# Queries projected in float32 and normalised at the output, no packing of the latents, own buffers for the gates' tanh

## The chip, the cores and the metric

The kernel runs on one core of one Trainium2 chip. The metric is the device time of one execution in microseconds (us). Several runs are timed, and one further execution is recorded by the hardware profiler; its rows are the views shown below. Engines are named as in the profile: PE is TensorE's matmul, PEld its weight load, DVE is VectorE, ACT is ScalarE, POOL is GpSimd, SP is SyncE. "SPq" and "ACTq" are the sequencers of SP and ACT that issue DMAs.

## The reference, cut to what matters

One backbone layer over 256 latent tokens and 256 context tokens: a SwiGLU FFN, two token mixers in parallel (a gated DeltaNet and a Mamba-2 SSD, each in both directions), their gated merge and an output projection, then a second FFN on the latents alone. The part that is changed is the queries and what uses them:

```python
qkv = jax.nn.silu(conv(qkv, gdn_conv_w))
q, k, v = jnp.split(qkv, [GDN_QK, 2 * GDN_QK], axis=-1)
q = l2norm(q.reshape(b, n, GDN_HEADS, GDN_DK)) * GDN_DK ** -0.5      # t * rsqrt(sum(t*t) + EPS)
k = l2norm(k.reshape(b, n, GDN_HEADS, GDN_DK))
...
qk = jnp.einsum('bnhid,bnhjd->bnhij', q, k) * decay                  # both uses of q are linear in it
q_in = q * jnp.exp(g)[..., None]
...
ya = (rmsnorm(o, gdn_norm_g) * jax.nn.silu(za)).astype(dt).reshape(b, n, GDN_V)
...
merged = jax.nn.sigmoid(ga) * (ya @ w_branch_gdn) + jax.nn.sigmoid(gb) * (yb @ w_branch_mb)
return merged @ w_out
```

The output o of a head and token is linear in that token's query, and rmsnorm then divides by the root of o's mean square plus EPS. So the query's norm can be left out if EPS is multiplied by 128 times (the query's sum of squares + EPS).

## The kernel before

Activations lie with channels on the 128 partitions and tokens along the row: NT = 512 tokens (256 context, then NL = 256 latent). A weight tile `raw` (128 x 1024 float32, four buffers, each loaded by SP) is used in one of two ways.

- **`proj`** (matmuls at lines 215, 216 and 217, "mm3"): ACT casts `raw` to `whi` (line 200), DVE takes the rest as `wlo` (line 204), and for each of 8 channel blocks PE runs three matmuls of type fp32r: hH x whi, hL x whi and hH x wlo. Keys, values, x (`wxs`) and the B matrices go this way over 512 tokens, queries over the 256 latents.
- **`projf`** (line 616): 8 matmuls in plain float32 on `hF`, straight from `raw`. The profile records each of them as two matmuls. The gates g (`wg`), C and zA go this way.

After a projection, `conv_silu` makes the convolution of five taps: a copy into `cbuf` and a scaled start on ACT, four steps on DVE (line 635), tanh on ACT (line 638), a last step on DVE (line 640). `l2` then normalises keys and queries: transposes to `l2t` (line 866), squares on ACT, sum on DVE (line 874, for the queries), the power on POOL (line 351), product `l2n` on DVE (line 877), transposes back to `l2b` (line 880), copy on ACT (line 881).

The middle of the program, from about 434 us on, is written as the list `PLAN` in `mixer` and reordered by a scheduler that goes by priorities (the numbers ahead of a slash) and its own simulated times; so each engine's order of instructions comes out of it and moves when any piece changes. Tiles of a tag share a fixed number of buffers: `tZ` holds the gates' `gth`, z's tanh tiles and the tiles `dtx` and `dte` of the time steps' softplus (`dts`, lines 741 to 754, 841 to 856); `tL` holds, among others, `dtz`, `dtg`, `rows_a` and `RB`.

The names in this stretch: `keys` (line 887 on) makes for each of the 8 heads the Gram matrix `pg` (PE, line 901), copies it to `kb` (ACT, line 903) and stores it by `Gsd<-kb` (SP, line 904); `N<-Gsd` (SP, line 910) reads blocks of it back, after every second head. `elim` multiplies N by the decay `D` (line 968) and inverts the triangular blocks in 30 steps on DVE (`etmp`, line 972, and `N`, line 975), stores them (`Tsd`, line 978), and `merge` reads them back as `TD` and `TT` (SP, line 1107) and begins with the transposes `pTx` (PE, line 1131). `merge` also needs decays `RA` and `RB`, loaded by SP (lines 1104 and 1112), subtracted on DVE (line 1119), exponentiated on ACT (line 1121) and multiplied into `Lm` on POOL (line 1122). The chain over chunks (`chain_step`), the queries, B and the x projections run between the merges.

Of the kernel before, what the change touches and what calls it, by code (L numbers as in the profile page):

```python
# [6 lines left out]
F32 = mybir.dt.float32  # L7
F32R = mybir.dt.float32r
AF = mybir.ActivationFunctionType
ALU = mybir.AluOpType  # L10
# [4 lines left out]
P = 128  # L15
D = 1024
KD = 8
NL = 256
NT = 512
FF = 2816  # L20
MF = 22
EPS = 1e-6
# [7 lines left out]
NCV = 2  # L30
POOLC = lambda t, s: False
PLAN = """10/k3 block_decay k6 5/elim 18/g5 13/dts 20/v2 g10 v7 13/m0 14/m1 13/chain_start s0 s1 m2 m3 22/q9
    B_part 27/x17 25/lat_h 22/C_part 30/zB5 g17 zA9 chain_out 13/s2 s3 14/gdn_norm 15/ssd_pre h40 51/y0 gdn_out y1 70/mb_out"""
NG = 5
GQ = 0
SSE = "gvg"
# [59 lines left out]
class Ks:  # L96

    def __init__(self, kern, nk, n, name, dt=F32R, lazy=False, tag="s4"):
        w = min(nk, 1024 // n)
        self.new = lambda: (kern.s4 if tag == "s4" else kern.tt)([P, w, n], name, dt)  # L100
        self.t = [None if lazy else self.new() for _ in range(-(-nk // w))]
        self.w = w

    def __getitem__(self, k):
        if self.t[k // self.w] is None:
            self.t[k // self.w] = self.new()
        return self.t[k // self.w][:, k % self.w]


class Packed:  # L110

    def __init__(self, t):
        self.t = t

    def __getitem__(self, k):
        j = k // 2
        return self.t[j // 2 * 2][:, k % 2, NL * (j % 2):NL * (j % 2) + NL]


class Ring:  # L120
# [19 lines left out]
class Kernel:  # L140
# [812 lines left out]
    @staticmethod  # L953
    def bc(ap, n, w):
        return ap.rearrange("p (h o) -> p h o", o=1).to_broadcast([ap.shape[0], n, w])
# [38 lines left out]
            self.tok_major(s, self.vsc[:, :, h].rearrange("t p c -> p t c"), "vt")  # L994
            yield

    def lat_h(self):

        nc = self.nc
        for i, X in enumerate((self.hH, self.hL)):  # L1000
            for j in (0, 2):
                dst, src = X.t[j][:, :, NL:NT], X.t[j + 1].bitcast(F32)[:, :, 0:NL]
                if i:
                    nc.vector.tensor_copy(dst, src)
                else:
                    nc.scalar.copy(dst, src)
        self.hH, self.hL = Packed(self.hH.t), Packed(self.hL.t)

    def q_gen(self):
        qT = self.qT = Ks(self, 8, NL, "qT", F32)  # L1010
        for h in range(8):
            acc = self.proj("wq", h, self.hH, self.hL, NL, QL[h % len(QL)])
            s = self.conv_silu(acc, NL, self.cwg[:, h])
            self.l2(s, NL, qT[h], 128.0, 128.0 * EPS)
            yield

    def xs_gen(self):
# [54 lines left out]
    def g_gen(self):  # L1072
        for m in range(16):
            acc = self.projf("wg", m)
            th = self.t2([P, NL], "gth", tag="tZ")
            self.nc.scalar.activation(th, acc, AF.Tanh, scale=0.5)  # L1076
            self.nc.scalar.dma_start(self.gsc[m], th)
            yield
# [187 lines left out]
    def gdn_norm(self):  # L1266

        nc, V = self.nc, self.nc.vector
        o, bc = self.o, self.bc
        rs = self.const([P, 2, 8], "ors")  # L1270
        for t in range(2):
            sq = getattr(self, OSQ)([P, 8, P], "osq")
            nc.scalar.activation(sq, o[t], AF.Square)
            V.tensor_reduce(out=rs[:, t], in_=sq, op=ALU.add, axis=AX.X)
        self.rsqrt(rs, rs, 1.0 / 128, EPS)
        for t in range(2):
            V.tensor_tensor(o[t], o[t], bc(rs[:, t], 8, P), op=ALU.mult)

# [354 lines left out]
```

## Time and profile before

| | us |
|---|---|
| three timed runs | 1347.86, 1344.52, 1350.04 (median 1347.86) |
| profiled execution, device time | 1350.37 |
| its span, first to last instruction | 1348.6 |
| mean granted TensorE clock | 0.973 |
| PE busy | 1267.5 (94%) |
| DVE busy | 977.1 (72%) |
| ACT busy | 508.9 (38%) |
| POOL busy | 172.4 (13%) |

The span is 1.8 us shorter than the device time of the same execution, and that execution is 2.5 us above the median of the timed runs. By the stages of the program: the first FFN until about 408 us; keys, gates, values and the elimination from 434 to 599.5 us (called stage B below); merges, chain, queries, B and x from 599.5 to 872 us (stage C); the SSD from 872 to 1004 us (stage D); gated output norms to 1056 us; branch and output projections and the second FFN to the end.

In the views, a row gives the line of the kernel's text, the engine, the operation and the tiles as out<-in, how often (x), busy time, and the idle time of the engine before it with what ended that wait.

### The profile page before, as it was taken

Reading aid. Unit: us, or ns where it says so; the run is one execution under the profiler, and the core shown is the slowest. Engines: PE = TensorE matmul, PEld = TensorE weight load, DVE = VectorE, ACT = ScalarE, POOL = GpSimd, SP = SyncE. Lnnn points to the kernel's source line nnn. Section 1 sums busy time; section 2 is a strip of 40 time slices with the busy share of each in tenths; the row PEclk is TensorE's granted clock in tenths of the full one; section 3 lists DMA queues with packets and bytes.
Section 4 is the critical chain, followed back from the end, with each engine's and each line's share of the span. In section 5 each row is a group of like instructions: output and inputs, shape, how many; then the busy total and the mean of one; then the engine's idle time right before and its main releaser. Section 6 shows DMA issues by size and latency. Waiting matters only on the chain.

```text
span 1348.6 us, 21052 instructions
## 1 busy us (share of the span) xinstructions
PE 1267.5 (94%) x8064; PEld 1083.8 (80%) x8064; DVE 977.1 (72%) x1692; ACT 508.9 (38%) x948; POOL 172.4 (13%) x130
## 2 busy tenths in 40 slices
PE   5889999999999997989998999998899899999997
PEld 3668888888899885779887888844468899999997
DVE  7998587646667966888778687997873466866565
ACT  3432122212236652345323565522223345544333
POOL 4200000000010231000122111333421001000000
PEclk9999999999999998999998999998999899999999
DMA  9256367636633398755542254554446556655552
GB/s 360 94 173 217 126 199 249 223 117 229 209 110 104 103 237 178 215 165 165 171 120 89 95 177 141 155 184 131 162 148 214 182 181 192 199 185 180 184 182 84
DMA packets 133016, 230.24 MB, mean 171 GB/s; under 512 B 46706, under 2 KB 78898, under 8 KB 132788
## 3 DMA queue, kind: packets, MB, share of 16 engines
q1 hardware_dynamic: 106240, 211.43, 49.7%
q10 hardware_dynamic: 26676, 17.47, 4.2%
q8 instruction: 63, 1.03, 0.3%
q14 instruction: 37, 0.30, 0.1%
HBM read 207.79 MB, written 21.07 MB: 170 GB/s over the span
## 4 chain that ended last, share of the span: by engine, by line
PE 63%; issue 17%; DVE 11%; DMA 7%; ACT 1%; POOL 1%; SPq 0%; ACTq 0%; DVEq 0%; POOLq 0%
PE acc L215 16%; PE acc L216 15%; PE acc L217 15%; PE acc L616 4%; PE acc L1054 2%; DVE junk L277 1%; DVE Es L1431 1%; DVE wlo L204 1%; PE pn L1232 1%; DMA zAsc<-zth 1%; DVE hL L440 1%; DMA Es<-asd 1%; DVE Es L1442 1%; PE pS L1258 1%; DMA raw<-in_wv 1%
## 5 line engine op out<-in xcount | busy, mean ns | idle before, releaser
L200 ACT CAST whi<-raw 128x1024 fp32r<-128x1024 f32 (+1 forms) x208 | 214.4, 1033 | 434.1 <-PE acc L216 369.4
L215 PE MATMUL acc<-hH,whi 128*128 128x512 f32 (+1 forms) x976 | 343.4, 358 | 17.2 <-ACT whi L200 8.3
L216 PE MATMUL acc<-hL,whi 128*128 128x512 f32 (+1 forms) x976 | 344.7, 355 | 4.6 <-DVE hL L440 4.6
L217 PE MATMUL acc<-hH,wlo 128*128 128x512 f32 (+1 forms) x976 | 343.3, 354 | 0.0
L204 DVE TENSOR_TENSOR wlo<-raw,whi 128x1024 fp32r<-128x1024 f32 (+1 forms) x208 | 254.4, 1225 | 93.3 <-ACT whi L200 92.0
L215 PEld LDWEIGHTS acc<-hH,whi 128*128 128x128 f32 x976 | 187.4, 192 | 43.0 <-ACT whi L200 8.6
L216 PEld LDWEIGHTS acc<-hL,whi 128*128 128x128 f32 x976 | 187.0, 192 | 30.5 <-DVE hL L440 6.9
L217 PEld LDWEIGHTS acc<-hH,wlo 128*128 128x128 f32 x976 | 186.3, 191 | 23.7
L277 DVE CUSTOM_DVE_ANT_0 junk<-wadat,cs 128x1024 f32<-128x1024 f32 x80 | 97.7, 1221 | 41.6 <-DMA wadat<-in_wadaT 40.9
L216 PE MATMUL acc<-aL,whi 128*128 128x256 f32 (+1 forms) x384 | 122.9, 323 | 0.0
L217 PE MATMUL acc<-aH,wlo 128*128 128x256 f32 (+1 forms) x384 | 122.3, 323 | 0.0
L215 PE MATMUL acc<-aH,whi 128*128 128x256 f32 (+1 forms) x384 | 122.3, 323 | 0.0
L616 PE MATMUL acc<-hF,raw 128*128 128x256 f32 x416 | 97.7, 391 | 14.6 <-ACT gth L1076 14.6
L635 DVE SCALAR_TENSOR_TENSOR cv<-cbuf,cc,cv 128x512 f32<-128x512 f32 (+1 forms) x144 | 102.0, 719 | 4.3 <-ACT cv L633 2.4
L616 PEld LDWEIGHTS acc<-hF,raw 128*128 128x128 f32 x416 | 80.3, 196 | 28.3 <-ACT gth L1076 16.0
L216 PEld LDWEIGHTS acc<-aL,whi 128*128 128x128 f32 x384 | 73.0, 190 | 5.7
L215 PEld LDWEIGHTS acc<-aH,whi 128*128 128x128 f32 x384 | 72.6, 190 | 5.7 <-DVE xc L572 0.2
L217 PEld LDWEIGHTS acc<-aH,wlo 128*128 128x128 f32 x384 | 72.7, 190 | 5.6
L382 POOL TENSOR_TENSOR sqa<-sqa,sqb 128x256 f32<-128x256 f32 x12 | 11.8, 981 | 430.5 <-ACT sqb L380 427.6
L572 DVE SCALAR_TENSOR_TENSOR xl<-acc,hg,xl 128x256 f32<-128x256 f32 x64 | 30.3, 481 | 47.3 <-PE acc L217 46.8
L1054 PE MATMUL acc<-raw,hF 128*128 128x512 f32 x128 | 59.4, 606 | 0.0
L1054 PEld LDWEIGHTS acc<-raw,hF 128*128 128x128 f32 x128 | 25.0, 197 | 30.2 <-issue 29.3
(398 smaller groups left out, 2082.3 us busy)
## 6 DMA issues: line engine op xcount, KB each, us to landing
raw<-in_wgu SPq DMA_DIRECT2D x76, 512.0 KB, 4.1
wadat<-in_wadaT SPq DMA_DIRECT2D x56, 512.0 KB, 4.1
raw<-in_wdn SPq DMA_DIRECT2D x44, 512.0 KB, 3.6
wada<-in_wada SPq DMA_DIRECT2D x16, 512.0 KB, 9.0
raw<-in_wg SPq DMA_DIRECT2D x16, 512.0 KB, 4.3
raw<-in_wxs SPq DMA_DIRECT2D x16, 512.0 KB, 3.4
Es<-asd SPq DMA_DIRECT2D x16, 512.0 KB, 4.3
raw<-in_wzB SPq DMA_DIRECT2D x16, 512.0 KB, 4.2
```

Source lines behind the costliest of these rows:

```text
L200: nc.scalar.copy(hi, raw)
L204: engs[i % len(engs)].tensor_tensor(lo[:, c:c + w], raw[:, c:c + w], hi[:, c:c + w].bitcast(F32), op=ALU.subtract)
L215: mm(acc, wh, xh, start=start, stop=False)
L216: mm(acc, wh, xl, start=False, stop=False)
L217: mm(acc, wl, xh, start=False, stop=stop)
L277: self.nc.vector.tensor_tensor_reduce(out=self.junk, in0=w, in1=self.cs[s], scale=1.0, scalar=0.0, op0=ALU.mult, op1=ALU.add, accum_out=out)
L440: nc.vector.scalar_tensor_tensor(out=hL[k][:, a:b], in0=u, scalar=sh[:, s:s + 1], in1=hH[k].bitcast(F32)[:, a:b], op0=ALU.add, op1=ALU.sub ...
L572: nc.vector.scalar_tensor_tensor(out=xs, in0=acc[:, NL * s - g0:NL * s - g0 + NL], scalar=hg[s][:, m:m + 1], in1=xs, op0=ALU.mult, op1=ALU ...
L616: self.nc.tensor.matmul(acc, w[:, k * P:k * P + P], self.hF[:, k], start=k == 0, stop=k == KD - 1)
L635: nc.vector.scalar_tensor_tensor(out=u3, in0=buf[:, 0:R, j:j + 64], scalar=cw[:, j:j + 1], in1=u3, op0=ALU.mult, op1=ALU.add)
L1054: nc.tensor.matmul(accs[t], self.hF[:, k, sl], w[:, wsl], start=k == 0, stop=k == 7)
L1232: nc.tensor.matmul(pn[:, j], TT[d][:, 4 * q + j], vt[q][:, j], start=True, stop=True)
```

## The change

- `q_gen` uses `projf` instead of `proj` (no `whi`, no `wlo`), writes the convolution's result straight into `qT`, and leaves `l2` out. In its place ACT squares `qT`, two matmuls against a column of ones give the sum of squares of each token (`pqs`), and ACT copies the two columns into `qs`.
- `gdn_norm` multiplies `qs` by 128 EPS, adds 128 EPS squared, adds the result to o's mean square, and POOL takes the power -1/2 as before.
- `lat_h` and `Packed` go: they copied the latents' halves of hH and hL into one tile, which the queries' projection alone read.
- `gth` leaves the tag `tZ` and gets two buffers of its own.

```diff
-    B_part 27/x17 25/lat_h 22/C_part 30/zB5 g17 zA9 chain_out 13/s2 s3 14/gdn_norm 15/ssd_pre h40 51/y0 gdn_out y1 70/mb_out"""
+    B_part 27/x17 22/C_part 30/zB5 g17 zA9 chain_out 13/s2 s3 14/gdn_norm 15/ssd_pre h40 51/y0 gdn_out y1 70/mb_out"""
...
-class Packed:
-
-    def __init__(self, t):
-        self.t = t
-
-    def __getitem__(self, k):
-        j = k // 2
-        return self.t[j // 2 * 2][:, k % 2, NL * (j % 2):NL * (j % 2) + NL]
...
-    def lat_h(self):
+    def q_gen(self):
 
         nc = self.nc
-        for i, X in enumerate((self.hH, self.hL)):
-            for j in (0, 2):
-                dst, src = X.t[j][:, :, NL:NT], X.t[j + 1].bitcast(F32)[:, :, 0:NL]
-                if i:
-                    nc.vector.tensor_copy(dst, src)
-                else:
-                    nc.scalar.copy(dst, src)
-        self.hH, self.hL = Packed(self.hH.t), Packed(self.hL.t)
-
-    def q_gen(self):
         qT = self.qT = Ks(self, 8, NL, "qT", F32)
+        self.qs = self.const([P, 2, 8], "qs")
         for h in range(8):
-            acc = self.proj("wq", h, self.hH, self.hL, NL, QL[h % len(QL)])
-            s = self.conv_silu(acc, NL, self.cwg[:, h])
-            self.l2(s, NL, qT[h], 128.0, 128.0 * EPS)
+            acc = self.projf("wq", h)
+            self.conv_silu(acc, NL, self.cwg[:, h], qT[h])
+            sq = self.t2([P, NL], "qsq")
+            nc.scalar.activation(sq, qT[h], AF.Square)
+            ps = self.smp([P, 2], "pqs")
+            for t in range(2):
+                nc.tensor.matmul(ps[:, t:t + 1], sq[:, t * P:t * P + P], self.ones[:, 0:1], start=True, stop=True)
+            nc.scalar.copy(self.qs[:, :, h], ps)
             yield
...
             acc = self.projf("wg", m)
-            th = self.t2([P, NL], "gth", tag="tZ")
+            th = self.tp.tile([P, NL], F32, tag="gth", bufs=2, name="gth")
             self.nc.scalar.activation(th, acc, AF.Tanh, scale=0.5)
...
-        self.rsqrt(rs, rs, 1.0 / 128, EPS)
+
+        e = self.const([P, 2, 8], "oeps")
+        V.tensor_scalar(out=e, in0=self.qs, scalar1=128 * EPS, scalar2=128 * EPS * EPS, op0=ALU.mult, op1=ALU.add)
+        V.scalar_tensor_tensor(out=rs, in0=rs, scalar=1.0 / 128, in1=e, op0=ALU.mult, op1=ALU.add)
+        mh = self.mhalf.rearrange("p (a o) -> p a o", o=1).to_broadcast([P, 2, 8])
+        nc.gpsimd.tensor_tensor(rs, rs, mh, op=ALU.pow)
```

From line 110 on, line numbers are lower by 10 in the changed text, and by 14 between `q_gen` and `gdn_norm`. Besides what the diff says, the scheduler gives every engine another order from the keys on. Three places matter for what follows.

On DVE, around the start of the elimination (`N<-N,D`), before. `cv` is a value's convolution, `dt`, `dte`, `dtx` and `dtg` belong to the softplus of the time steps, `etmp` and `N` are the elimination:

```order
L751 SCALAR_TENSOR_TENSOR dt<-dt,dtz 128x256
L968 TENSOR_TENSOR N<-N,D 128x1024 x2
L635 SCALAR_TENSOR_TENSOR cv_3344<-cbuf_3238,cc,cv_3344 128x512
L752 SCALAR_TENSOR_TENSOR dt<-dt,dte 128x256
L972 TENSOR_TENSOR etmp<-N 128x60
L635 SCALAR_TENSOR_TENSOR cv_3344<-cbuf_3238,cc,cv_3344 128x512
L754 SCALAR_TENSOR_TENSOR dt<-dt,dtx 128x256
L975 TENSOR_TENSOR N<-N,etmp 128x2x30
L845 TENSOR_TENSOR dtg<-dt,alogs 128x256
L972 TENSOR_TENSOR etmp<-N 128x116
L975 TENSOR_TENSOR N<-N,etmp 128x2x29x2
L640 SCALAR_TENSOR_TENSOR cv_3344<-cv_3344 128x512
```

The same place of the changed kernel (`gt` is the last copy of `dts`, `RB` the first merge's decay):

```order
L843 COPY gt<-pcd 128x256
L625 SCALAR_TENSOR_TENSOR cv_3343<-cbuf_3237,cc,cv_3343 128x512
L1105 TENSOR_TENSOR RB<-gcA,RB 128x256
L625 SCALAR_TENSOR_TENSOR cv_3343<-cbuf_3237,cc,cv_3343 128x512
L1105 TENSOR_TENSOR RB<-RB,gcA 128x256
L625 SCALAR_TENSOR_TENSOR cv_3343<-cbuf_3237,cc,cv_3343 128x512 x2
L1105 TENSOR_TENSOR RB<-gcA,RB 128x256
L630 SCALAR_TENSOR_TENSOR cv_3343<-cv_3343 128x512
L1105 TENSOR_TENSOR RB<-RB,gcA 128x256
L625 SCALAR_TENSOR_TENSOR cv_3344<-cbuf_3238,cc,cv_3344 128x512 x4
L630 SCALAR_TENSOR_TENSOR cv_3344<-cv_3344 128x512
L958 TENSOR_TENSOR N<-N,D 128x1024 x2
```

The rest of the softplus, its copies `gc` and `gt`, the whole of two convolutions and two of three pairs of `RB` now stand ahead of the elimination, where before they stood inside it; behind `N<-N,D` come sixteen rows of `etmp` and `N` alone. In all, twelve convolution steps of line 635 stand inside the elimination instead of fourteen, one pair of `RB` instead of three, and six `wlo` as before.

On PE, from the values' first transposes (`ptm`) to the first merge's `pTx`, before. `acc<-hF,raw` are the gates' matmuls, and behind x48 come 120 matmuls of values:

```order
L985 MATMUL ptm<-ident,cv_3343 128x128 x4
L616 MATMUL acc<-hF,raw 128x256 x16
L848 MATMUL pcd<-dtg,UT 128x4x32
L848 MATMUL pcd<-dtg,LT 128x4x32
L849 MATMUL pcd<-dtg,ones 128x256
L616 MATMUL acc<-hF,raw 128x256 x8
L855 MATMUL prow<-ident,gc 128x128
L616 MATMUL acc<-hF,raw 128x256 x48
...
L985 MATMUL ptm<-ident,cv_3344 128x128 x4
L985 MATMUL ptm<-ident,cv_3343 128x128 x4
L1131 MATMUL pTx<-ident,TD 32x32 x8
```

And of the changed kernel, where behind x74 come the same 120 matmuls of values, and then 20 more:

```order
L891 MATMUL pg<-kT 128x128 x4
L606 MATMUL acc<-hF,raw 128x256 x4
L975 MATMUL ptm<-ident,cv_3343 128x128 x4
L606 MATMUL acc<-hF,raw 128x256 x74
...
L975 MATMUL ptm<-ident,cv_3343 128x128 x4
L975 MATMUL ptm<-ident,cv_3344 128x128 x4
L205 MATMUL acc<-hH_3012,whi 128x512
L206 MATMUL acc<-hL_3014,whi 128x512
...
L206 MATMUL acc<-hL_3098,whi 128x512
L975 MATMUL ptm<-ident,cv_3343 128x128 x3
L1117 MATMUL pTx<-ident,TD 32x32 x8
```

`pcd` and `prow` of the softplus have moved up, ahead of the last `pg`, and 20 of the 24 matmuls of the last value's projection, which stood behind `pTx`, stand ahead of it.

On SP, from the sixth head's store of the Gram matrix to the last read of N, before (these are the DMAs that SP issues, in their order):

```order
L904 DMA Gsd<-kb_3352 128x4x128
L606 DMA raw<-in_wg 128x1024
L910 DMA N<-Gsd 16x64x32 x2
L904 DMA Gsd<-kb_3350 128x4x128
L1196 DMA kTt<-kTsc 128x1024 x2
L904 DMA Gsd<-kb_3351 128x4x128
L910 DMA N<-Gsd 16x64x32 x2
```

And of the changed kernel:

```order
L894 DMA Gsd<-kb_3352 128x4x128
L1098 DMA RB<-gsd 64x8x32 x4
L900 DMA N<-Gsd 16x64x32 x2
L1098 DMA RB<-gsd 64x8x32 x2
L894 DMA Gsd<-kb_3350 128x4x128
L1098 DMA RB<-gsd 64x8x32 x2
L1182 DMA kTt<-kTsc 128x1024 x2
L894 DMA Gsd<-kb_3351 128x4x128
L900 DMA N<-Gsd 16x64x32
L596 DMA raw<-in_wg 128x1024
L900 DMA N<-Gsd 16x64x32
```

Eight loads of `RB` have moved up between the last three stores of the Gram matrix, and a load of weights stands between the two halves of the last read of N.

## The prediction

> **What bounds the kernel now.** I read the table of engines first (in the table above: PE 94% of the span, DVE 72%), then busy time by stage, the waits of the stage with most idle PE time, and the chain of work through that stage.
>
> Busy time in four stretches (stage B, C, D, and the gated norms). The columns are start:end, length, then busy time and count of PE, PEld, DVE, ACT and POOL, the granted clock, the DMA share and GB/s:
>
> ```profile
> core 0: us, PE busy (x) PEld busy (x) DVE busy (x) ACT busy (x) POOL busy (x), PEclk, DMA share, GB/s
> 434.00:599.50 165.50, 146.98 (x718) 124.45 (x717) 130.97 (x241) 75.96 (x209) 25.58 (x16) 0.96 0.68 178
> 599.50:872.00 272.50, 265.61 (x2505) 234.54 (x2506) 211.94 (x394) 125.36 (x259) 49.31 (x37) 0.97 0.46 140
> 872.00:1004.00 132.00, 121.08 (x381) 65.58 (x381) 111.29 (x208) 35.23 (x82) 49.96 (x36) 0.91 0.47 155
> 1004.00:1056.00 52.00, 44.53 (x227) 39.52 (x227) 17.65 (x34) 14.74 (x30) 5.78 (x5) 0.91 0.57 182
> ```
>
> PE idles 18.5 us in B, 6.9 in C, 10.9 in D. The queries lie in C, where DVE is busy 212 of 272.5 us and ACT 125: there only work on PE is on the path. The gates' tanh and the time steps lie in B. Who waits there (waiting instruction <- what it waited for: us in total, times, longest):
>
> ```profile
> PE acc L616 <- ACT gth L1076: 14.6, 4, 9.3
> ACT gth L1076 <- DVE dt L752: 12.7, 1, 12.7
> DVE dte L742 <- DMA gsc<-gth: 5.8, 1, 5.8
> ```
>
> These are one loop through the shared tag: the softplus waits for a gate's buffer to be stored, then the gate's tanh waits for the softplus to give its buffer back, and PE waits for the tanh. But 14.6 us of waiting is not 14.6 us of time. The chain through the end of B (start, duration, what; rows left out between):
>
> ```profile
> 515.21 0.33 SPq L1196
> ...
> 516.11 5.01 DMA Gsd<-kb
> 521.17 4.66 DMA N<-Gsd
> ...
> 527.49 2.36 DVE N L968 x2
> ...
> 591.55 5.07 DMA Tsd<-N
> ...
> 597.01 2.49 DMA TD<-Tsd
> 599.54 0.91 PE pTx L1131 x16
> ```
>
> The first merge's `pTx` ends the stage. It waits for the elimination on DVE (527.5 to 591.5 us), which waits for the last head's Gram matrix. PE's waits on `gth` lie beside that. So B gets shorter only if the elimination starts sooner or takes fewer microseconds, and the order of DVE's instructions decides that.
>
> **The change part by part.**
>
> *Queries in float32 (stage C, PE).* The spacing of fp32r matmuls of 256 columns, and a whole float32 projection:
>
> ```profile
> 619.78 0.28 PE L215 MATMUL acc<-hH,whi 128*128 128x256 f32 x1
> 619.90 0.28 PE L216 MATMUL acc<-hL,whi 128*128 128x256 f32 x1
> ...
> 875.04 3.45 PE acc L616 x16
> ```
>
> A head had 24 x 0.12 = 2.88 us; it gets 8 float32 matmuls, recorded as 16, in 3.45 us. That is +0.57 us a head, **+4.6 us** for eight, on PE in a stage where PE is the bound. So this part alone costs time.
>
> The Trainium skill, "FP8 and Floating Point Precision", section TensorE Precision Notes, says that true float32 takes four passes through the array. By it a head would take 8 x 4 x 0.12 = 3.84 us, and the part +7.7 instead of +4.6 us, an estimate. The trace has 3.45 / (8 x 0.12) = 3.6 passes, and I go by the trace.
>
> *No `l2`, no split for the queries.* What goes from DVE is above all `wlo`:
>
> ```profile
> L204 DVE TENSOR_TENSOR wlo<-raw,whi 128x1024 fp32r<-128x1024 f32 (+1 forms) x208 | 254.4, 1225 | 93.3 <-ACT whi L200 92.0
> ```
>
> Eight of them are 9.8 us of DVE, with eight casts on ACT and the norm's small steps on four engines. None of it holds PE in C by the idle times above, so I take 0. On PE a head loses four transposes and gains two matmuls with one column, recorded as four. The nearest row is the four transposes of values in 1.04 us, below: between 0 and -0.5 us a head, if the new ones cost nothing. I take 0, and -3.5 us as the lower end. `lat_h` goes with four small copies that nobody waited for: 0. The norm's two more DVE instructions of 16 columns stand at the end of D before a POOL power that stood there already: 0, at most +1.
>
> *The elimination (stage B, DVE).* DVE's groups from 527 to 592 us (count | busy, mean ns | idle before):
>
> ```profile
> L635 DVE SCALAR_TENSOR_TENSOR cv<-cbuf,cc,cv 128x512 f32<-128x512 f32 x14 | 12.4, 888 | 0.0
> L1119 DVE TENSOR_TENSOR RB<-gcA,RB 128x256 f32<-128x256 f32 x3 | 2.3, 777 | 1.5 <-DMA RB<-gsd 1.5
> L640 DVE SCALAR_TENSOR_TENSOR cv<-cv 128x512 f32<-128x512 f32 x2 | 1.4, 680 | 0.0
> L1119 DVE TENSOR_TENSOR RB<-RB,gcA 128x256 f32<-128x256 f32 x3 | 1.3, 420 | 2.2 <-DMA RB<-gsd 2.2
> L851 DVE COPY gc<-pcd 128x256 f32<-128x256 f32 x1 | 0.4, 423 | 0.5 <-PE pcd L849 0.5
> L853 DVE COPY gt<-pcd 128x256 f32<-128x256 f32 x1 | 0.4, 414 | 0.0
> L845 DVE TENSOR_TENSOR dtg<-dt,alogs 128x256 f32<-128x256 f32 x1 | 0.4, 411 | 0.0
> L752 DVE SCALAR_TENSOR_TENSOR dt<-dt,dte 128x256 f32<-128x256 f32 x1 | 0.4, 410 | 0.0
> L754 DVE SCALAR_TENSOR_TENSOR dt<-dt,dtx 128x256 f32<-128x256 f32 x1 | 0.4, 410 | 0.0
> ```
>
> and one convolution step among them, beside POOL's work:
>
> ```profile
> 529.35 2.72 POOL L1122 TENSOR_TENSOR Lm<-Lm,RA 64x1024 f32<-64x1024 f32 x1 [26.79 <-DMA Lm<-Gsd]
> ...
> 529.77 2.85 DVE L635 SCALAR_TENSOR_TENSOR cv<-cbuf,cc,cv 128x512 f32<-128x512 f32 x1
> ```
>
> By the new order these leave the stretch: the five rows of `dts`, 2.1 us and 0.5 of wait; two of fourteen `cv` steps, the one of 2.85 and one of (12.4 - 2.85) / 13 = 0.73; one L640, 0.7; four of six `RB`, (2.3 + 1.5 + 1.3 + 2.2) x 4/6 = 4.9. Together 11.7 us. The six `wlo` stay. POOL's `Lm` still runs beside the elimination and will stretch another DVE instruction by 2.85 - 0.73 = 2.1 us, so I take **-9.6 us**; ends: -11.7 if it stretches none, -7.1 if the waits for `RB` stay with the pair that is left.
>
> The Trainium skill, "SBUF — State Buffer", section Who interferes with whom, says that a DVE instruction with two inputs in SBUF contends with a GpSimd instruction that reads SBUF. By it the 2.1 us do come back, since `etmp` and `N` read two tiles from SBUF. The trace agrees with its 2.85 us instead of 0.73, and without the return the sum would be 2.1 us lower.
>
> *Its start.* Rows on PE ahead of the last `pg`, of the value matmuls' spacing, and of a group of `ptm`:
>
> ```profile
> 487.00 1.97 PE L616 MATMUL acc<-hF,raw 128*128 128x256 f32 x4 [2.78 <-ACT gth L1076]
> ...
> 567.77 0.23 PE acc L215
> 568.00 0.23 PE acc L216
> ...
> 600.45 1.04 PE ptm L985 x4
> ```
>
> Ten value matmuls more (2.3 us), two of `hF` more (16 records in 3.45 us: 0.9) and `pcd` and `prow` (about 0.9, by the four transposes' 1.04) stand ahead of the last `pg`; the wait of 2.8 us at 487 goes, as gates have their own buffers: **+1.3 us**. Ends: -1.2, if the other short waits on `gth` (14.6 - 9.3 - 2.8 = 2.5) go too, and +4.1, if none goes. The softplus moves too: DVE has it between the keys' convolutions, where it was idle 34.5 us of B.
>
> *Can PE keep up?* From the last `pg` to `pTx` PE now has 80 gate matmuls (160 records, 34.5 us), 140 of values (x 0.23 = 32) and 19 transposes (4.9): 71.4 us, from about 515, so until 586.4. The shorter elimination lets `pTx` start at 599.5 - 9.6 + 1.3 = 591.2. PE is ready 4.8 us before, which is also the most that its waits on ACT may last (tanh now stands behind exponentials of `RA` and `RB` in ACT's order).
>
> *The last value.* 20 of its 24 matmuls, 20 x 0.23 = **-4.6 us**, leave C, where PE is the bound, for PE's wait at the end of B.
>
> Sum: +4.6 - 9.6 + 1.3 - 4.6 = -8.3 us. Against the profiled execution's 1350.4 that is 1342.1; the median of the timed runs is 2.5 us below that execution, so **1339.6 us**.
>
> **The rivals.**
>
> *A late last Gram matrix (the other side).* On SP, eight loads of `RB` now stand between the last three stores `Gsd`, and on ACT the exponentials of `RB` stand ahead of the last copies `kb`. `RB` lies in tag `tL` with `rows_a`, so its first load waits for the softplus to be over and `rows_a` stored:
>
> ```profile
> asd<-rows_a ACTq DMA_DIRECT2D x1, 64.0 KB, 3.8
> RB<-gsd SPq DMA_DIRECT2D x12, 64.0 KB, 4.2
> ...
> 544.38 2.77 SPq L1112 DMA_DIRECT2D RB<-gsd  x4
> ```
>
> If none of it is hidden, the elimination starts 3.8 + 4.2 + 2 x 2.77 = 13.5 us later: 1353.1 us. From 8.3 us of slip on the kernel is slower than before. For it: SP had no slack there, since the last store (516.11) followed two loads `kTt` at 515.21 at once. Against: the softplus and its copies, some 20 instructions of 0.41 us or 8.2 us of DVE, have the idle time of DVE in B, and the loads need no more than to be issued during the two heads before.
>
> *PE stays the bound in B.* If the gates' tanh wait as long as before (in ACT's order, not for buffers), the shorter elimination meets a PE that comes no sooner, and the queries are paid in full: 1350.4 + 4.6 - 2.5 = 1352.5. For it: the elimination's `wlo` need `whi`, whose buffers PE gives back, so DVE falls in with PE. Against: the longest wait (9.3 us) is put down to the buffer.
>
> *More comes back.* -11.7, the start at -1.2 and the transposes at -3.5: 2.1 + 2.5 + 3.5 below the forecast, 1331.5. For it: DVE and ACT have less to do in C; against: PE waits for them so little there.
>
> **How the numbers follow.** The measurement tells 0.5% from no change, 6.7 us: faster is below 1341.1, slower above 1354.6. Forecast 0.50 (its own range 1334 to 1346; three quarters of it below 1341), more comes back 0.17, PE the bound 0.17 (a sixth of it above 1354.6), late Gram matrix 0.16 (more than half above, as slips add up). Faster 0.38 + 0.17 = 0.55; slower 0.03 + 0.09 = 0.12; same 0.33. The range takes in the ends of both sides: 1329 to 1353.
>
> **What would show it.** Waits of PE on `gth` gone or under 5 us; 51 to 57 us from the first `N<-N,D` to `Tsd<-N` instead of 64; that `N<-N,D` at 526 to 532; a query's projection 3.45 us; PE busy in C longer by no more than 1 us. It is wrong if the elimination starts after 537, or if PE, not `TD<-Tsd`, is last at the first `pTx`.

## The result and the profile after

| | before | changed |
|---|---|---|
| median of 11 runs each, us | 1349.89 (1344.52 to 1356.79) | 1356.47 (1352.89 to 1363.14) |
| ratio, with 95% interval | | 1.0051 (1.0036 to 1.0067) |
| second series, on another chip | 1348.46 | 1359.5, ratio 1.0067 (1.0044 to 1.0089) |

The change makes the kernel 7 to 9 us slower, where 8 us faster was forecast; the time lies above the range. (A ratio can differ from the quotient of the two medians by about 0.0015; gains and losses below go by the ratios, since the runs come from several chips.) The profiled execution of the changed kernel took 1363.14 us, the longest of its eleven; a second profile of it (experiment 5) has a span of 1359.0 instead of 1361.4 us and shows what differs from one execution to the next.

The same middle of the program, cut on TensorE at the same events in each kernel: from the transposes `pab` to the first `pTx` (B), to the first `pSs` of the SSD (C), to the last matmul on `ya`, the first branch's projection (the rest). Columns as in the prediction: window, length, busy time of PE, PEld, DVE, ACT and POOL, PEclk, DMA share, GB/s. Before:

```profile
434.80:599.50 164.70, 146.18 (x712) 123.65 (x709) 130.77 (x240) 75.29 (x207) 25.58 (x16) 0.96 0.68 179
599.50:867.90 268.40, 261.51 (x2490) 231.68 (x2491) 207.88 (x388) 124.14 (x257) 45.21 (x35) 0.97 0.46 139
867.90:1073.50 205.60, 187.21 (x762) 125.46 (x762) 144.49 (x262) 57.98 (x121) 59.84 (x43) 0.92 0.52 169
```

Changed:

```profile
433.80:599.80 166.00, 152.64 (x740) 128.64 (x739) 131.21 (x245) 75.21 (x208) 22.93 (x16) 0.97 0.67 178
599.80:882.70 282.90, 273.23 (x2405) 238.56 (x2405) 193.28 (x351) 114.98 (x250) 42.31 (x27) 0.93 0.44 133
882.70:1086.20 203.50, 182.69 (x758) 121.29 (x757) 142.15 (x260) 56.92 (x118) 63.09 (x43) 0.93 0.50 168
```

Length less PE busy is PE's idle time: 18.5, 6.9 and 18.4 us before; 13.4, 9.7 and 20.8 after. In B PE has 6.5 us more work, above all the matmuls of the last value that were moved there, and waits only 5.2 us less, so B does not get shorter. C gets 14.5 us longer: 2.8 us of idle time, and 11.7 us in which PE is busy. That is the clock: (1 - 0.93) x 282.9 = 19.8 us of it is lost there, against (1 - 0.97) x 268.4 = 8.1 before. DVE has 14.6 us less to do in C and nothing comes of it.

*Stage B.* DVE, the changed kernel's start of the elimination (start, duration, instruction, idle before):

```profile
533.87 2.36 DVE L958 TENSOR_TENSOR N<-N,D 128x1024 f32<-128x1024 f32 x2 [9.38 <-DMA Lm<-Gsd]
```

The last `pg` on PE, and ACT up to its copy:

```profile
515.74 1.05 PE L891 MATMUL pg<-kT 128*128 128x128 f32 x8
```

```profile
520.05 1.28 ACT L1107 ACTIVATE RB<-RB 32x512 f32<-32x512 f32 x2 [2.78 <-DVE RB L1105]
521.35 0.59 ACT L893 COPY kb<-pg 128x512 f32<-128x512 f32 x1
```

SP's issues, of the last Gram matrix, the last read of N, and the way back from the elimination:

```profile
521.96 0.37 SPq L894 DMA_DIRECT2D Gsd<-kb  x1
524.26 0.60 SPq L900 DMA_DIRECT2D N<-Gsd  x1
524.92 0.65 SPq L596 DMA_DIRECT2D raw<-in_wg  x1
525.62 0.59 SPq L900 DMA_DIRECT2D N<-Gsd  x1
...
588.86 0.33 SPq L968 DMA_DIRECT2D Tsd<-N  x1
592.76 2.23 SPq L1093 DMA_DIRECT2D TD<-Tsd  x4
```

The elimination takes 588.9 - 533.9 = 55.0 us instead of 591.5 - 527.5 = 64.0, as forecast. But it starts 6.4 us later than before instead of 1.3. (The row puts its wait down to a load of `Lm`; in `after_chg`, below, the same row names the reads `N<-Gsd` that it needs.) The last `pg` itself comes 3.0 us later (515.74 instead of 512.73), and its copy 7.2 (521.35 instead of 514.15), as it stands behind two exponentials of `RB` on ACT, which wait for DVE and its loads.

From `Tsd` to `pTx` it is 599.8 - 588.9 = 10.9 us instead of 8.0, and here the elimination is no longer what ends the stage. PE, at its last wait in B and at `pTx`:

```profile
594.65 0.50 PE L205 MATMUL acc<-hH,whi 128*128 128x512 f32 x1 [0.45 <-ACT cv L623]
...
599.76 0.69 PE L1117 MATMUL pTx<-ident,TD 32*32 32x32 f32 x16
```

Before, PE stood 1.8 us at the first `pTx` until `TD` came. Now it is busy from 594.65 on with the matmuls of the last value and comes to `pTx` without a wait. The four loads of `TD` were issued by 594.2 and took at most 3.8 us to land, so `TD` was there by 598.0. PE comes last, and an elimination that ended sooner would not by itself have moved this `pTx`.

PE's longest waits in B are these:

```profile
PE acc L606 <- ACT gth L1062: 4.4, 2, 4.0
PE acc L606 <- DMA raw<-in_wg: 3.5, 2, 2.2
```

*Stage C.* What PE waited for, before and (below) after:

```profile
PE acc L215 <- ACT cv L633: 3.0, 1, 3.0
PE pTa L1153 <- ACT TD L1146: 1.9, 1, 1.9
PE pTx L1131 <- DMA TD<-Tsd: 1.8, 1, 1.8
```

```profile
PE pS L1244 <- DVE ch L1220: 4.3, 3, 3.1
PE pTx L1117 <- DMA TT<-Tsd: 3.6, 1, 3.6
PE pS L1244 <- ACT o L1236: 1.7, 1, 1.7
```

Two new waits stand early in the stage, for `TT` and for `ch`. For `TT`, SP shows why: the load that PE waits for stands behind three loads of the chain's first step (`ch`), and the first of those waits 3.4 us for the store of a value, the fourth of eight, which ACT issued at 595.1.

```profile
600.42 0.34 SPq L1199 DMA_DIRECT2D ch<-vsc  x1
600.80 0.91 SPq L1203 DMA_DIRECT2D ch<-ksc  x2
601.75 0.43 SPq L1093 DMA_DIRECT2D TT<-Tsd  x1
```

The clock goes where PE has been idle. The changed kernel around its wait for `ch`, then before around its longest wait in C (columns as above):

```profile
652.00:656.00 4.00, 2.68 (x14) 2.07 (x13) 1.77 (x4) 1.22 (x3) 0.11 (x1) 1.00 1.00 228
656.00:664.00 8.00, 5.50 (x27) 5.02 (x28) 7.74 (x11) 1.72 (x6) 5.96 (x3) 0.57 0.52 153
664.00:672.00 8.00, 8.00 (x81) 7.36 (x79) 5.37 (x11) 3.05 (x6) 0.00 (x0) 0.50 0.65 164
```

```profile
728.00:732.00 4.00, 1.65 (x13) 1.22 (x11) 3.91 (x4) 1.91 (x7) 3.74 (x2) 1.00 0.03 6
732.00:740.00 8.00, 5.84 (x14) 4.69 (x15) 7.93 (x10) 1.50 (x3) 5.04 (x4) 0.57 0.54 197
```

In both, the clock is full when the wait begins and half behind it: 8 x (1 - 0.57) = 3.4 us lost before; in the changed kernel 3.4 and then 4.0 more while PE is busy all the time. So a wait is paid a second time.

The Trainium skill, "TensorE: Matmul & The Clock Gate", Part 1, says that the clock halves after an idle window of about 3.4 us and comes back after a busy one, and that the windows run freely, so that the loss differs between executions. The trace agrees in kind: 3.4 us lost at half clock are 6.9 us at half clock, about two such windows, and two executions of the changed kernel lose 10.3 and 6.7 us in the same place (experiment 5). The mean granted clock is 0.972 to 0.984 in the profiles below.

### The profile page after: what moved, and what is told of

The parts are those of the page before. It is cut to its first block, busy times and chain, and to the rows that moved or that the text cites. A ratio compares the mean times of both kernels' runs of the same rounds, so it can differ in the third digit from the quotient of the medians.

```text
span 1361.4 us, 20828 instructions
## 1 busy us (share of the span) xinstructions
PE 1279.9 (94%) x8000; PEld 1089.5 (80%) x8000; DVE 961.7 (71%) x1659; ACT 498.7 (37%) x938; POOL 169.9 (12%) x122
## 5 line engine op out<-in xcount | busy, mean ns | idle before, releaser
L190 ACT CAST whi<-raw 128x1024 fp32r<-128x1024 f32 (+1 forms) x200 | 206.1, 1033 | 447.4 <-PE acc L206 351.3
L205 PE MATMUL acc<-hH,whi 128*128 128x512 f32 (+1 forms) x912 | 322.8, 361 | 12.9 <-ACT whi L190 8.3
L206 PE MATMUL acc<-hL,whi 128*128 128x512 f32 (+1 forms) x912 | 326.7, 360 | 5.8 <-DVE hL L430 5.8
L207 PE MATMUL acc<-hH,wlo 128*128 128x512 f32 (+1 forms) x912 | 324.5, 358 | 0.0
L194 DVE TENSOR_TENSOR wlo<-raw,whi 128x1024 fp32r<-128x1024 f32 (+1 forms) x200 | 242.5, 1214 | 90.9 <-ACT whi L190 89.2
L205 PEld LDWEIGHTS acc<-hH,whi 128*128 128x128 f32 x912 | 173.8, 191 | 38.4 <-ACT whi L190 8.6
L206 PEld LDWEIGHTS acc<-hL,whi 128*128 128x128 f32 x912 | 174.4, 192 | 32.3 <-DVE hL L430 8.9
L207 PEld LDWEIGHTS acc<-hH,wlo 128*128 128x128 f32 x912 | 174.3, 191 | 23.5
L606 PE MATMUL acc<-hF,raw 128*128 128x256 f32 x544 | 132.5, 400 | 10.7 <-ACT gth L1062 4.4
L606 PEld LDWEIGHTS acc<-hF,raw 128*128 128x128 f32 x544 | 107.3, 201 | 29.8 <-issue 6.1
L372 POOL TENSOR_TENSOR sqa<-sqa,sqb 128x256 f32<-128x256 f32 x12 | 11.7, 979 | 429.8 <-ACT sqb L370 348.9
```

Of the source, the lines that this page charges most:

```text
L190: nc.scalar.copy(hi, raw)
L194: engs[i % len(engs)].tensor_tensor(lo[:, c:c + w], raw[:, c:c + w], hi[:, c:c + w].bitcast(F32), op=ALU.subtract)
L205: mm(acc, wh, xh, start=start, stop=False)
L206: mm(acc, wh, xl, start=False, stop=False)
L207: mm(acc, wl, xh, start=False, stop=stop)
L372: (nc.gpsimd if SQE[nst] == "g" else nc.vector).tensor_tensor(a[:, 0], a[:, 0], q, op=ALU.add)
```

## The experiments

Fourteen runs, each timed against the kernel before on the same chip in five rounds. Three theories stood at first: the gain is lost in B, where the last Gram matrix comes late, and the queries are paid in C (A); the loss comes from the buffers (B); the buffers gain what was forecast and the queries lose more (C).

**1 to 4: the change taken apart.** Own buffers alone (`gth_only`):

```diff
-            th = self.t2([P, NL], "gth", tag="tZ")
+            th = self.tp.tile([P, NL], F32, tag="gth", bufs=2, name="gth")
```

> The kernel before with own buffers for the gates' tanh and nothing else; all engines stand in the order of the changed kernel up to the first merge. Theory A (the changed kernel lost its gain because the last Gram matrix and the reads behind the elimination came late, and pays in C for the queries): the elimination takes 54 to 56 us instead of 64 but starts at 532 to 535 and the first pTx at 598 to 601; no gain and no loss by itself, 1346 to 1354. Rival B (the buffers carry the loss, the queries are free): 1355 to 1358. Rival C (the buffers gain what was forecast and the queries lose more than that): 1338 to 1344.

Measured: 1339.64, ratio 0.9929 (0.9904 to 0.9954). As rival C has it, this part gains 9.6 us. Its three stages:

```profile
434.50:603.10 168.60, 153.97 (x743) 128.91 (x741) 134.87 (x248) 77.74 (x212) 23.89 (x16) 0.97 0.69 182
603.10:855.10 252.00, 248.50 (x2427) 221.26 (x2427) 197.96 (x370) 117.43 (x244) 51.98 (x36) 0.98 0.46 140
855.10:1066.10 211.00, 192.10 (x797) 130.75 (x796) 148.04 (x270) 61.92 (x130) 55.77 (x42) 0.93 0.51 168
```

B is 3.9 us longer than before, and its first `pTx` comes at 603.1. The gain is not where it was forecast: PE works 7.8 us more in B and 4.9 more in the last stage, C is left with 13.0 less, and idles 3.5 us instead of 6.9.

The queries alone (`q_only`; the changed kernel with `gth` back in `tZ`):

```diff
-            th = self.tp.tile([P, NL], F32, tag="gth", bufs=2, name="gth")
+            th = self.t2([P, NL], "gth", tag="tZ")
```

> The changed kernel with the gates' tanh back in the shared buffers; all engines stand in the order of before up to the first merge, and the queries are as changed. Theory A: the whole loss is here, 1354 to 1359. Rival B: 1347 to 1352, no change. Rival C: 1360 or more. The prediction's working for this part alone (a query's projection +0.57 us, nothing else): +4.6, 1354.

Measured: 1352.0, ratio 1.0015 (0.9998 to 1.0033): about +2 us, at most 4.5, so a little less than the +4.6 that were forecast for this part, and neither what A nor what C needs. So the parts by themselves would give 0.9929 x 1.0015 = 0.9944 together; the changed kernel has 1.0051. None of the three had that.

Float32 alone, normalisation kept (`qf_l2`; packing out, own buffers out):

```diff
-            acc = self.proj("wq", h, self.hH, self.hL, NL, QL[h % len(QL)])
+            acc = self.projf("wq", h)
```

> The kernel before with the queries' projection alone in float32 (packing out, normalisation kept, gates' buffers shared): the price of float32 by itself. By the spacing of matmuls +4.6 us, 1353 to 1356. If the relief of DVE and ACT pays for it: 1348 to 1352. If float32 brings the clock or a wait with it: 1357 or more.

Measured: 1358.0, ratio 1.0057 (1.0030 to 1.0084). The +4.6 us lie in the interval; so does twice as much, and the median is where a wait or the clock was to come on top.

No normalisation alone, split projection and packing kept (`q_split`):

```diff
-            s = self.conv_silu(acc, NL, self.cwg[:, h])
-            self.l2(s, NL, qT[h], 128.0, 128.0 * EPS)
+            self.conv_silu(acc, NL, self.cwg[:, h], qT[h])
+            sq = self.t2([P, NL], "qsq")
+            nc.scalar.activation(sq, qT[h], AF.Square)
...
```

> The kernel before with the queries left unnormalised alone (projection split as before, packing kept, gates' buffers shared): the price of leaving the normalisation out. If only work off PE goes: no change, 1347 to 1352, and with four transposes a head against two matmuls of one column at most 3.5 us faster. If the loss in C comes from here (new order, the queries' sums): 1353 or more.

Measured: 1335.04, ratio 0.9886 (0.9859 to 0.9912), 15 us faster. No theory had expected that from work that PE hardly waited for.

**5 to 8: the same work in other orders.** The changed kernel once more (`after_again`, unaltered):

> The changed kernel once more, unaltered, for a second profile. In the first one TensorE's granted clock was lost for 10.2 us at 657 to 678 us, more than anywhere else. If this belongs to the kernel (the waits of the chain's start ahead of it bring it on): again 8 us or more within 650 to 690, time 1354 to 1360. If it was chance: 5 us or less there, and a profiled execution about 6 us shorter than 1363, with the same median.

Measured: 1359.5, ratio 1.0067. From 656 to 680 us the second profile has a mean clock of 0.72 instead of 0.57: 24 x 0.28 = 6.7 us lost instead of 10.3, between the two marks. C is 7 us shorter than in the first. Two of PE's waits in C, and the stage:

```profile
PE pS L1244 <- DVE ch L1220: 4.3, 2, 4.0
PE pTx L1117 <- DMA TT<-Tsd: 4.2, 1, 4.2
```

```profile
601.40:877.00 275.60, 265.06 (x2406) 231.64 (x2405) 193.89 (x351) 114.85 (x250) 41.93 (x27) 0.96 0.46 137
```

So some 7 us of the first profile's C, in its clock, come and go between executions of the same kernel. The waits for `TT` and `ch` belong to the kernel. In this profile too PE comes to the first `pTx` without a wait.

Own buffers and no normalisation, without float32 (`gth_split`: the diffs of `gth_only` and `q_split`):

> Own buffers for the gates' tanh and queries left unnormalised, but their projection split as before (packing kept): the changed kernel without its float32. Theory A (float32 in the queries costs 17 us with either order, and the two other parts add up): 1335 - 10 = 1325, 1322 to 1329. Rival B (own buffers do not get on with unnormalised queries, as the loss of the changed kernel against the one with shared buffers suggests): 1335 to 1343.

Measured: 1338.95, ratio 0.9912 (0.9889 to 0.9936). Two gains of 9.6 and 15 us give 12 together: rival B by the number, though not for its reason, as the next runs show.

One number of the plan in the changed kernel (`after_q28`):

```diff
-    ... s0 s1 m2 m3 22/q9
+    ... s0 s1 m2 m3 28/q9
```

> The changed kernel with one number of the plan changed, the queries' priority 28 instead of 22: the same instructions, in another order behind the first merge. Theory A (the price of float32 is TensorE time, +4.6 us, and what the order makes of it): the time moves by 4 us or more, either way; below 1352 if the order with early queries is what held up the chain. Rival (float32 itself costs the 17 us, by clock or weights, wherever it stands): 1355 to 1359.

Measured: 1351.66, ratio 1.0020 (0.9999 to 1.0041), where the unaltered one on the same chip had 1.0067. Theory A: six microseconds, by the order alone.

Five more matmuls in each query's projection (`q_split_pad`, on `q_split`):

```diff
+            for j in range(5):
+                nc.tensor.matmul(acc, wh[:, 0:P], self.hH[j][:, 0:NL], start=True, stop=True)
```

> Shared buffers, unnormalised queries, projection split, and 5 more matmuls of the same kind in each query's projection, whose results are overwritten: 5 x 0.12 = 0.6 us more on TensorE for a head, as float32 takes. Theory A (only TensorE time counts): 1335 + 4.8 = 1340, 1337 to 1342. Theory B (any change of length gives another order, and the order decides): 1344 or more, or 1334 or less. With float32 in its place the kernel took 1352.

Measured: 1346.79, ratio 0.9980 (0.9962 to 0.9999): some 12 us more than `q_split`, for 4.8 us of matmuls. Theory B. The scheduler gave every engine another order behind the first merge.

**9 to 12: the order, and two single waits.** The plan's number alone, on `q_split` (`q_split_q28`) and on the kernel before (`before_q28`), the same edit as in `after_q28`:

> Unnormalised queries with their projection split as before (the kernel of 1335 us), with the queries' priority in the plan 28 instead of 22: the same instructions in another order behind the first merge. Theory A (the order behind the first merge is worth several us either way, and most of the 15 us of gain was a good order): 4 us or more slower, 1339 or more. Rival B (the gain is that of the work left out): 1332 to 1338.

> The kernel before, with the queries' priority 28 instead of 22 and nothing else: the same instructions in another order. Theory A (order alone is worth several us): 3 us or more off 1350, either way. Rival B (the orders that the scheduler gives are worth the same, and work decides): 1347 to 1353.

Measured: `q_split_q28` 1354.6, ratio 1.0028 (1.0007 to 1.0049) against 0.9886; `before_q28` 1355.11, ratio 1.0040 (1.0019 to 1.0060). Theory A in both: the 15 us of `q_split` were a good order. With the number 28 in both, leaving the normalisation out is worth 1.0028 against 1.0040, some 2 us, within the noise. The middle of `q_split` and that of `q_split_q28`, with the same instructions:

```profile
436.40:1059.90 623.50, 588.27 (x3963) 476.00 (x3962) 477.66 (x864) 255.05 (x585) 126.69 (x85) 0.97 0.55 163
```

```profile
435.60:1079.50 643.90, 598.28 (x3963) 482.73 (x3962) 481.03 (x864) 256.29 (x585) 126.75 (x85) 0.95 0.53 158
```

Counts are equal. Idle time is 35.2 us in the one and 45.6 in the other, and PE is busy 10.0 us longer with the same matmuls, since the clock is lower. Half of the 20 us are waits, and half is the clock.

The wait for `TT` (`after_chg`): the chain's first loads go to GpSimd's queue, the same for `kt`.

```diff
-                nc.sync.dma_start(vt[q], self.vsc[t, :, hqs[q]])
+                (nc.gpsimd if s == 0 else nc.sync).dma_start(vt[q], self.vsc[t, :, hqs[q]])
```

> The changed kernel, with the eight loads of the chain's first step issued by GpSimd instead of SP, so that the last load of TT no longer stands behind them; all other engines keep their order but for 2 to 22 rows. Theory A (PE's wait of 3.8 to 4.4 us for TT at 602 us, and the clock lost behind it, are time): the wait is gone, -4 to -7 us, 1350 to 1354. Rival B (the wait only takes the place of another at the chain's start, the one of 3 to 4 us for ch at 655): that one grows, and the time stays, 1356 to 1359.

Measured: 1349.72, ratio 0.9992 (0.9974 to 1.0011), 8 to 10 us less than the changed kernel, with some 4 us either way. Theory A, and more than the wait's 4 us. What PE waits for in C, and the stage:

```profile
PE pS L1244 <- DVE ch L1220: 3.8, 2, 2.6
PE pn L1218 <- ACT S L1246: 2.4, 1, 2.4
PE pS L1244 <- ACT o L1236: 0.8, 1, 0.8
```

```profile
603.60:869.70 266.10, 259.14 (x2404) 227.04 (x2404) 193.88 (x352) 114.92 (x250) 46.06 (x35) 0.99 0.47 142
```

The wait for `TT` is gone and the one for `ch` has not grown. Against the second profile C loses 3.6 us of idle time, and PE is busy 5.9 us less, by a clock of 0.99 instead of 0.96.

A buffer for `rows_a` (`after_rows`):

```diff
-        rw = self.t2([P, P], "rows_a", tag="tL")
+        rw = self.tp.tile([P, P], F32, tag="rwa", bufs=1, name="rows_a")
```

> The changed kernel, with a buffer of its own for rows_a, so that the loads of RB need not wait for its store; all engines keep their order but for two to eight rows each around these loads. Theory A (the first rival of the prediction came true: loads and exponentials of RB hold back the last Gram matrix): the loads of RB are issued in 3 us instead of 5 to 6, the first N<-N,D starts 2 to 4 us earlier than 534 to 536, and the kernel gains 2 to 4 us, 1353 to 1356. Rival B (the last N is late for another reason, the load of weights between its halves): N at 533 to 536 as before and no gain, 1356 to 1359.

Measured: 1357.35, ratio 1.0049 (1.0030 to 1.0068), no gain; the first `N<-N,D` starts at 537.6 us, later than either theory had it. SP issues the four loads of `RB` that used to take 5 to 6 us in 3.0, but still late, and the last Gram matrix is stored at 524.5:

```profile
508.70 3.02 SPq L1098 DMA_DIRECT2D RB<-gsd  x4
...
523.61 0.82 SPq L1182 DMA_DIRECT2D kTt<-kTsc  x2
524.52 0.38 SPq L894 DMA_DIRECT2D Gsd<-kb  x1
```

The wait that the prediction's first rival named, for the store of `rows_a`, is not what starts the elimination late.

**13 and 14: what was open then.** `q_split` with `after_chg`'s edit (`q_split_chg`), in which PE, DVE and ACT keep `q_split`'s order row for row:

> Unnormalised queries with their projection split as before (the kernel of 1335 us), with the eight loads of the chain's first step issued by GpSimd instead of SP; PE, DVE and ACT keep their order to the row. In this kernel PE did not wait for TT. Theory A (moving these loads gained 8 to 10 us in the changed kernel because it took away the wait for TT and the clock lost behind it): nothing to gain here, ratio to before 0.985 to 0.992, as without it. Rival B (these loads are better on GpSimd in any case): 5 us or more faster than without, ratio 0.984 or less.

Measured: 1339.07, ratio 0.9928 (0.9906 to 0.9951). Nothing gained, rather 4 to 6 us lost, just outside the range of theory A: rival B is out, the loads are no better on GpSimd by themselves.

`after_chg` with the first merge's loads of `RB` on GpSimd too (`after_rbg_chg`):

```diff
-                nc.sync.dma_start(RB[r0:r0 + 64, 8 * d:8 * d + 8], ...)
+                (nc.gpsimd if s == 0 else nc.sync).dma_start(RB[r0:r0 + 64, 8 * d:8 * d + 8], ...)
```

> The changed kernel with the chain's first loads and also the first merge's eight loads of RB issued by GpSimd. PE, DVE and ACT keep their order but for 2 to 26 rows. Theory A (SP's queue, with the loads of RB between the stores of the Gram matrix, is what starts the elimination late): the first N<-N,D at 532 or earlier instead of 534 to 538, and 2 to 5 us below the kernel with the chain's loads alone, ratio to before 0.995 to 0.998. Theory B (ACT holds back the last Gram matrix, whose copy stands behind the exponentials of RB): N at 534 to 538 still, ratio 0.998 to 1.001.

Measured: 1356.69, ratio 1.0055 (1.0033 to 1.0077), 8.5 us more than `after_chg`. Neither theory had that, but the run shows what late loads of `RB` do. In the trace four of them are issued by POOL. POOL's loads, DVE, ACT, SP, and PE's longest wait in B:

```profile
505.72 0.91 POOL L1098 DMA_DIRECT2D RB<-gsd  x1 [0.66 <-PE pcd L839]
513.24 0.71 POOL L1098 DMA_DIRECT2D RB<-gsd  x1 [6.61 <-issue]
518.31 0.68 POOL L1098 DMA_DIRECT2D RB<-gsd  x1 [4.36 <-issue]
522.75 0.69 POOL L1098 DMA_DIRECT2D RB<-gsd  x1 [3.76 <-issue]
```

```profile
528.49 0.42 DVE L1105 TENSOR_TENSOR RB<-RB,gcA 128x256 f32<-128x256 f32 x1 [8.48 <-DMA RB<-gsd]
...
544.33 2.36 DVE L958 TENSOR_TENSOR N<-N,D 128x1024 f32<-128x1024 f32 x2 [7.66 <-DMA N<-Gsd]
```

```profile
528.95 1.28 ACT L1107 ACTIVATE RB<-RB 32x512 f32<-32x512 f32 x2 [13.25 <-DVE RB L1105]
```

```profile
534.01 0.37 SPq L894 DMA_DIRECT2D Gsd<-kb  x1
```

```profile
531.75 1.09 PE L975 MATMUL ptm<-ident,cv 128*128 128x128 f32 x4 [8.68 <-DVE cv L630]
```

GpSimd issues the loads 4.4 to 7.5 us apart. ACT waits 13.25 us ahead of an exponential that the last Gram matrix does not need (528.95 instead of 516.37 in `after_chg`); the store of that matrix goes out at 534.0 instead of 524.4, and the elimination starts at 544.3 instead of 536.4. So the copy of the last `pg`, behind the exponentials of `RB` on ACT, sets the start of the elimination.

The kernel pays 8.5 us, but not shown is that it pays at the elimination. DVE waits 8.48 us for `RB` with a value's convolution behind it, and PE waits 8.68 us for that convolution, 1.4 in `after_chg`. B ends at 611.7 instead of 603.6, with 7.4 us more of idle time on PE, and in both kernels PE comes to the first `pTx` without a wait.

What the exponentials behind that copy would give was not tried. What float32 costs with the order held was not reached either, for the order changes with every edit of PE's work. With unnormalised queries, the six kernels in float32 that differ in order or buffers have ratios of 0.9992 to 1.0067, the five split ones 0.9886 to 1.0028.

The best kernel measured is `q_split`, 1.1% faster than before, and by `q_split_q28` it owes that to its order.

## Why the prediction was wrong, point by point

Two steps failed: that PE would be ready in B (forecast for the stage: -9.6 + 1.3 = -8.3 us; measured: +1.3), and that C would stay as it was (forecast: 0; measured: +14.5, and +7.2 in the second profile).

- **A query's projection, 3.45 us, +4.6 us in all.** Not contradicted: `qf_l2` has +4 to +11 us, and in `q_only`, where the last value stays in C, PE is busy 266.2 us in C instead of 261.5. In the changed kernel this and the last value's -4.6 leave PE's work in C where it was.
- **No normalisation: 0, at best -3.5 us.** 15 us faster in one order and 4 slower in another. The step failed in taking for granted that leaving out work off the path leaves the path as it is. The scheduler made another order of all engines behind the first merge, and the time went by that order, from -15 to +4 us. At an equal number of the plan (`q_split_q28`, `before_q28`) the work itself is worth some 2 us, within the noise.
- **The elimination, -9.6 us.** 55.0 us instead of 64.0: -9.0. Right.
- **Its start, +1.3 us.** +6.4 (533.87 against 527.49), and +7.7 in the second profile. The step counted PE's work ahead of the last `pg` (+3.0 us instead of 1.3) and left out what stands ahead of its copy on ACT (4.2 us more); the rows were in the order and only a rival had them. The first rival was right about the place (ACT's exponentials ahead of the last Gram matrix), wrong about the reason (`after_rows`).
- **Can PE keep up? Ready 4.8 us before `pTx`.** This is the step that failed in B. PE's work from the last `pg` to `pTx` was sized rightly, 72.5 us instead of 71.4. But PE waited 10.6 us in that stretch, where at most 4.8 were allowed: 4.0 for `gth`, 3.5 for `raw`, the rest for convolutions and copies of values. So PE came last at the first `pTx`, a sign of being wrong that the prediction names, and B took 166.0 us instead of the 156 that were forecast. The second rival, that PE stays the bound in B, was right about this and wrong about the reason: the waits for `gth` did fall. How much of these waits goes back to the late loads and exponentials of `RB` stays open.
- **From `Tsd` to `pTx`, taken as before.** 10.9 us instead of 8.0, as PE was not ready.
- **The last value in B's cover, -4.6 us.** The matmuls moved there, and there was no cover: PE came last. It idles 13.4 us in B, and 14.6 in `gth_only`, not the 5.6 that the forecast left (18.5 - 9.6 + 1.3 - 4.6). The waits for `gth` fell from 14.6 to 4.4 us (7.1 in the second profile), but 3.5 us of new ones for `raw` came.
- **C otherwise, 0.** This term, put at nothing, and B's together turned the sign: C took 14.5 us more, 7.2 in the second profile. The waits for `TT` and `ch` were not in any rival, though the first could be read from SP's order: `TT` behind `ch<-vsc`, which needs a value's store. `after_chg` gives the price, 8 to 10 us for a wait of 4; behind it the clock falls.
- **What was to show it.** Of five marks, the length of the elimination and a query's 3.45 us came as forecast (20 records in 4.48 us at full clock; behind the wait for `TT` 16 took 5.94), and the `gth` waits in one profile of two. `N<-N,D` came at 533.9 instead of 526 to 532, and PE's time in C grew by 11.7 us (3.6 in the second profile) instead of 1. Of the two signs of being wrong, PE was last at the first `pTx`; the other, a start after 537, did not come in the changed kernel's two profiles. The sum of two parts that were each about right alone (-12.9 forecast and -9.6 measured for the buffers; +4.6 and +2 for the queries) was wrong together.

## What to carry to other kernels

Where a scheduler sets the order, an edit is two changes, the work and a new order; change only a number of the plan once or twice, and know how far the order alone moves the time (here 5 to 19 us), before a gain or loss of that size is put down to the work. Read the new order on the in-order queues for what stands ahead of the last item of the chain that ends a stage: here two exponentials ahead of a copy, and three loads, one of which waits for a store, ahead of the load that PE waits for. When a chain gets shorter, look which engine comes last at its end: work that is moved under a wait makes that engine the last. A wait of a matrix engine that is busy nine tenths of the time can cost about twice its length, as the clock falls behind it.

## What the runs showed of the hardware

- Behind waits of PE of 1.9 to 4.2 us the granted clock stood at half, at full work too: before, from 668 to 672 us, 4 x (1 - 0.57) = 1.7 us lost behind a wait of 1.9 (`pTa`); in the changed kernel 3.4 us and more behind the wait for `ch`. One drop there, at 684 to 688 us with a clock of 0.57, follows no wait, so the waits are not the whole rule. Two kernels with the same instructions differ by 10.4 us of idle time and 10.0 us of matmul time (`q_split`, `q_split_q28`). The lines of the two: span and mean clock.

```profile
core 0: 1335.1 us, clock 0.980
```

```profile
core 0: 1354.6 us, clock 0.972
```

- Loads of 64 KB issued by GpSimd went out 4.4 to 7.5 us apart with nothing in the profile that they waited for, where SP takes 0.69 us for each (2.77 for four).
